# First output projection as seven block products, two chains of weight sums that begin behind x, and a last normalisation on three engines

## The chip, the cores and the metric

One core of a Trainium2 chip runs the kernel. The metric is the device time in microseconds (us) of one execution. Engines: PE (TensorE, matmuls), DVE (VectorE), ACT (ScalarE), POOL (GpSimd) and SP (SyncE, which here only issues transfers). Each engine carries out its own instructions in the order of the program; between engines they wait on semaphores. A transfer (DMA) is issued by an engine, waits there for what it depends on, and then runs on 16 DMA engines that all queues share.

## The reference

Two layers over x (512 tokens by 2048 channels), float32; each ends with `x <- LayerNorm(alpha*x + mixer(x))`.

```python
# layer 0 (even): attention half and Mamba-2 (SSD) half, then one output projection
hcat = x @ w_in
y_att = rms_norm(diff_attention(q, k, v, lam), subln_g) * (1 - lam_init) * silu(g_att)   # 1024 channels
y = ssd_chunked(xs * dt, a * dt, b, c) + d_skip * xs
y_ssm = rms_norm(y * silu(z), per group of 512) * ssm_norm_g                              # 1024 channels
y0 = concatenate([y_att, y_ssm]) @ w_out            # 512x2048 by 2048x2048: the first output projection
# layer 1 (odd): pooling mixer over four channel groups
y1 = (grouped(pool(v)) + b_grp) * scale * silu(g) @ w_out2                                # the second one
```

## The kernel before

Every float32 product is split: a value is written as `hi + lo` (line 113: ACT copies `hi` rounded to fp32r, DVE subtracts to get `lo`), and `mm3` (line 103) issues three matmuls, hi\*hi, hi\*lo, lo\*hi. Weights come as units of 128x1024 (512 KB): `unit` (line 117) loads one from SP's queue into one of three `raw` buffers and splits it; it is placed ahead of its program position by a priority. A scheduler then sets each engine's final order from its own model of times; the order of the text is only its priority.

Stages, in order: the B/C block of the SSD input (its results are the four tiles `bc`); projections of the token-major columns in five groups (`xs_group`, line 220); eight blocks of `xs` with the SSD steps woven in; the gate z; `ssm_norm` (line 445) scales y by `rs`, a reciprocal root that POOL computes with a power (line 452), and PE transposes the scaled y; eight attention heads; the first output projection (lines 611 to 700); `ln1`; the pooling mixer in four groups; the second output projection as seven block products instead of eight (lines 878 to 953); `finish`, the last LayerNorm.

Work beside the matmuls is fed by lanes: generators that yield estimated microseconds, advanced by each `mm3`.

The seven products of the second projection need sums of weight blocks. `presum` (line 191) makes them by transfers alone, on POOL's queue: it loads a block into `t`, adds others by accumulating transfers, and stores the four sums T1 to T4 to DRAM; a second tile `t3` makes T3. One call issues 10 transfers of 512 KB (2 loads, 4 accumulating, 4 stores); 8 calls make 80. `PACE` (7.0) is what each step yields to `lane3`.

The first output projection before is plain: 4 column groups of 512, 8 units each, 4 token tiles, 2 contraction blocks per unit, three matmuls each: 4 x 8 x 4 x 2 x 3 = 768 matmuls of 512 columns, into the tiles `po`.

`finish(t)` (line 922): two DVE operations per 512 columns (lines 926, 928), then a store by SP.

Of the kernel before, what the change touches and what calls it, by code (L numbers as in the profile page):

```python
# [29 lines left out]
PACE = 7.0  # L30
# [57 lines left out]
def hybrid_trunk(ctx: ExitStack, tc: tile.TileContext, xT, xtok, wa, wg, wo, prm, con, lnp, out, dbg=None):  # L88
# [6 lines left out]
    lane, lane2, lane3 = Lane(), Lane(), Lane()  # L95
# [7 lines left out]
    def mm3(o, sh, sl, mh, ml, start, stop, more=False):  # L103

        nc.tensor.matmul(o, sh, mh, start=start, stop=False, skip_group_check=more)  # L105
        nc.tensor.matmul(o, sh, ml, start=False, stop=False, skip_group_check=more)  # L106
        nc.tensor.matmul(o, sl, mh, start=False, stop=stop, skip_group_check=more)  # L107
        us = 3 * mh.free_size() / 2400.0
        lane.tick(us)
        lane2.tick(us)  # L110
        lane3.tick(us)
# [74 lines left out]
    def wsrc(c, j, cp, ch):  # L186
        return wo[((cp * 2 + c) * 2 + j) * 4 + ch]

    tsum = {}

    def presum(cp, ch, pool):
# [10 lines left out]
        nc.gpsimd.dma_start(t, wsrc(0, 1, cp, ch), accum_op=ALU.add)  # L202
        nc.gpsimd.dma_start(t3, wsrc(1, 1, cp, ch), accum_op=ALU.add)
# [4 lines left out]
        nc.gpsimd.dma_start(t, wsrc(1, 1, cp, ch), accum_op=ALU.add)  # L208
# [3 lines left out]
        nc.gpsimd.dma_start(t, wsrc(1, 0, cp, ch), accum_op=ALU.add)  # L212
# [5 lines left out]
    with ExitStack() as l1:  # L218
# [14 lines left out]
        with ExitStack() as sd:  # L233
# [207 lines left out]
        a2 = l1.enter_context(tc.tile_pool(name="att2", bufs=2))  # L441
# [157 lines left out]
        lane3.flush()  # L599
        yh, yl = newT("y")  # L600

        def y_ready(k):
            if k < 8:
                if k >= 6:
                    lane.flush()
                split(yh[k], yl[k], yTa[0][:, k])
            else:
                split(yh[k], yl[k], yTs[:, k - 8])


        un = next_units(32)
        ks = list(range(8, 16)) + list(range(8))
        first = [bank("mm", f"po{t}") for t in range(NT)]
        for u in range(8):
            hi, lo = unit(un[u])
            for j in range(2):
                y_ready(ks[2 * u + j])
            for t in range(NT):
                for j in range(2):
                    k = ks[2 * u + j]  # L620
                    mm3(first[t], yh[k][:, ts(t)], yl[k][:, ts(t)], hi[:, j * 512:(j + 1) * 512],
                        lo[:, j * 512:(j + 1) * 512], u + j == 0, u == 7 and j == 1)
        if dbg is not None and "yTa" in dbg:
            nc.sync.dma_start(dbg["yTa"], yTa[0])
            nc.sync.dma_start(dbg["yTs"], yTs)

    def out_mm(pt, t, u, ah, al, ks, hi, lo):
        for j in range(2):
            k = ks[2 * u + j]
            mm3(pt, ah[k][:, ts(t)], al[k][:, ts(t)], hi[:, j * 512:(j + 1) * 512],  # L630
                lo[:, j * 512:(j + 1) * 512], u + j == 0, u == 7 and j == 1)

    def out_cols(toks, units, ah, al, ks, evac):

        pt = {t: bank("mm", f"po{t}") for t in toks}
        for u in range(8):
            hi, lo = unit(units[u])
            for t in toks:
                out_mm(pt[t], t, u, ah, al, ks, hi, lo)
                if u == 7:  # L640
                    evac(t, pt[t])

    def moments(pool, stt):
        mv = pool.tile([P, 2], F32, tag="mv", name="mv", bufs=4)
        nc.vector.bn_aggr(mv, stt)
        rstd = pool.tile([P, 1], F32, tag="rstd", name="rstd", bufs=4)
        nc.vector.tensor_scalar(rstd, mv[:, 1:2], EPS, None, op0=ALU.add)
        nc.gpsimd.tensor_tensor(rstd, rstd, nhalf[:, :1], ALU.pow)
        return mv[:, 0:1], rstd

    def cs(cg):
        return slice(cg * 512, (cg + 1) * 512)

    with ExitStack() as l2:
        x1p = l2.enter_context(tc.tile_pool(name="x1p", bufs=1))
        x1h = [x1p.tile([P, 4, T], F32R, tag=f"h{k}", name=f"x1h{k}") for k in range(4)]
        x1l = [x1p.tile([P, 4, T], F32R, tag=f"l{k}", name=f"x1l{k}") for k in range(4)]
        oc = l2.enter_context(tc.tile_pool(name="oc", bufs=1))
# [3 lines left out]
        zp = zs.enter_context(tc.tile_pool(name="zp", bufs=2))  # L662
# [4 lines left out]
        def evac1(cg):  # L667
            def ev(t, pt):
                xs = xp[t][:, cs(cg)]
                nc.vector.scalar_tensor_tensor(xs, in0=xs, scalar=ALPHA, in1=pt, op0=ALU.mult, op1=ALU.add)  # L670
                nc.vector.bn_stats(stt[t][:, cg], xs)
            return ev
# [51 lines left out]
        v0 = act.tile([P, 4, T], F32, tag="l2", name="v0")  # L724
        gts = act.tile([P, 4, T], F32, tag="h2", name="gt0")
# [7 lines left out]
        H0, H1 = slice(0, 256), slice(256, 512)  # L733

        with ExitStack() as mix:
            p2 = mix.enter_context(tc.tile_pool(name="pool2", bufs=2))
            yr = []
            x1d = dram.tile([NT, P, D], F32, name="x1d")

            def residual():  # L740

                for cg in range(4):
# [4 lines left out]
                    for t in range(NT):  # L747
# [3 lines left out]
                        nc.gpsimd.dma_start(x1d[t][:, cs(cg)], xs)  # L751
# [3 lines left out]
            for g, w in enumerate(WINDOWS):  # L755
                plh = act.tile([P, 4, T], F32R, tag="h3", name="plh")
                pll = act.tile([P, 4, T], F32R, tag="l3", name="pll")
# [35 lines left out]
                yr.append(act.tile([P, 2, 2, T], F32, tag=("h0", "l0", "h1", "l1")[g], name=f"yr{g}"))  # L793
# [24 lines left out]

        op = l2.enter_context(tc.tile_pool(name="op", bufs=1))
        xp = [x1p.tile([P, D], F32, tag=f"h{t}", name=f"xq{t}") for t in range(NT)]
# [4 lines left out]
        def combo(pool, tags, src):  # L830

            hi, lo = (pool.tile([P, 8, 256], F32R, tag=t, name=f"c{t}") for t in tags)
            for g in range(4):
                q = slice(2 * g, 2 * g + 2)
                split(hi[:, q], lo[:, q], src(g, q))
            return hi, lo
# [4 lines left out]
        def summed(first, second, sub):  # L841
            def src(g, q):
                o = sraw[:, q]
                nc.vector.tensor_tensor(o, first(g, q), second(g, q), ALU.subtract if sub else ALU.add)
# [7 lines left out]

        def prod(o, a, b, ch, start, stop):

            for i in range(2):
                for uu in range(2):
                    u = 2 * ch + uu
                    mm3(o[i], a[0][:, u, ts(i)], a[1][:, u, ts(i)], b[0][:, uu * 512:(uu + 1) * 512],
                        b[1][:, uu * 512:(uu + 1) * 512], start and u == 0, stop and u == 7, True)

        def col(cp, j):
            return cs(2 * cp + j)

        def acc(t, cp, j, pt, sub=False, done=False):
            xs = xp[t][:, col(cp, j)]
# [3 lines left out]

        def pair(tag):  # L870
            if tag == "mm":
                return [bank("mm", "pY") for _ in range(2)]
            if tag == "aux":
                return [bank("aux", "pZ") for _ in range(2)]
            b = bank2("pZ2")
            return [b[:, 0], b[:, 1]]
# [3 lines left out]
        for cp in range(2):  # L880
            for ch in range(4):
                prod(Y[cp], a11, unit(wsrc(0, 0, cp, ch)), ch, True, False)
                prod(Z[cp], s1, unit(tsum[1, cp, ch]), ch, True, False)
            if cp == 0:
                s2 = combo(x1p, ("l0", "l1"), summed(sr, A11, True))
# [150 lines left out]
```

## Time and profile before

| | |
|---|---|
| median of 3 runs | 1440.17 us (1436.61 to 1444.72) |
| profiled execution, its time | 1442.42 us |
| its span (first to last instruction) | 1439.9 us |
| PE busy | 1409.6 us (98%) |
| DVE busy | 818.7 us (57%) |
| ACT busy | 548.5 us (38%) |
| POOL busy | 96.6 us (7%) |

The page gives busy time by engine, 40 slices of the span, the transfers by queue, the chain that ended last, the costliest groups and the transfers by line. Windows, timelines, waits and the transfers of a stretch are then asked of the trace. A matmul's duration in a row (0.39 us) overlaps the next one's; the distance between two starts is what one costs in a dense stretch. "idle before" in brackets is how long the engine had nothing to do, and what it waited for.

### The profile page before, as it was taken

What the parts mean: (1) busy time and instruction counts of PE and PEld (TensorE: products, weight loads), DVE (VectorE), ACT (ScalarE), POOL (GpSimd) and SP (SyncE); (2) the same over time, 40 slices, a digit from 0 to 9 for tenths busy, and PEclk for the clock granted to TensorE, in tenths of its full rate; (3) what the DMA queues carried; (4) which work ended last, traced back from release to release, by engine and by line L of the source; (5) the groups of instructions that cost most, each with busy time, mean ns of one, the idle gap of its engine ahead of it and who ended that gap; (6) DMA issues with size and microseconds to landing.
All of it is one profiled execution on the core that took longest, in us unless ns stands there. A gap on an engine that the chain in (4) does not pass through costs nothing.

```text
span 1439.9 us, 17608 instructions
## 1 busy us (share of the span) xinstructions
PE 1409.6 (98%) x6893; PEld 1192.2 (83%) x6893; DVE 818.7 (57%) x1198; ACT 548.5 (38%) x906; POOL 96.6 (7%) x150
## 2 busy tenths in 40 slices
PE   8999999999999999999999999999999999999994
PEld 6898899888888888888888889978888888888883
DVE  4755764542555555557335677865445346476678
ACT  4332433432544444446223456323232232345440
POOL 1112111110000000000000000110000000200101
PEclk9999999999999999999999999999999999999997
DMA  9999867763222222222545555663333333466764
GB/s 326 268 270 248 226 175 198 190 174 104 88 84 78 80 82 80 82 82 80 159 134 148 190 176 167 216 210 109 94 96 99 94 101 99 145 225 192 244 203 150
DMA packets 65266, 221.97 MB, mean 154 GB/s; under 512 B 7584, under 2 KB 7712, under 8 KB 65184
## 3 DMA queue, kind: packets, MB, share of 16 engines
q1 hardware_dynamic: 49824, 166.32, 36.6%
q0 software_dynamic: 15360, 54.53, 14.3%
q8 instruction: 54, 0.88, 0.2%
q14 instruction: 28, 0.23, 0.0%
HBM read 195.66 MB, written 25.17 MB: 153 GB/s over the span
## 4 chain that ended last, share of the span: by engine, by line
PE 91%; DVE 4%; DMA 3%; issue 1%; ACT 1%; SPq 0%; POOL 0%; DVEq 0%; ACTq 0%; POOLq 0%
PE pg L107 8%; PE pg L105 8%; PE pg L106 8%; PE po L107 4%; PE po L105 4%; PE po L106 4%; PE pv L107 3%; PE pv L106 3%; PE pv L105 3%; PE pq L107 2%; PE pq L105 2%; PE pgt L107 2%; PE pk L107 2%; PE pk L106 2%; PE pq L106 2%; PE pxs L105 2%
## 5 line engine op out<-in xcount | busy, mean ns | idle before, releaser
L115 DVE TENSOR_TENSOR lo<-raw,hi 128x1024 fp32r<-128x1024 f32 (+3 forms) x298 | 353.9, 1188 | 421.3 <-ACT hi L114 419.5
L114 ACT CAST hi<-raw 128x1024 fp32r<-128x1024 f32 (+3 forms) x298 | 304.9, 1023 | 581.8 <-PE po L107 97.0
L105 PE MATMUL pg<-hi,xh 128*128 128x346 f32 (+2 forms) x320 | 114.9, 360 | 0.0
L107 PE MATMUL pv<-x1h,lo 128*128 128x512 f32 (+1 forms) x320 | 111.9, 350 | 2.4 <-DVE lo L115 2.4
L105 PE MATMUL pv<-x1h,hi 128*128 128x512 f32 (+1 forms) x320 | 112.0, 350 | 0.0
L106 PE MATMUL pg<-lo,xh 128*128 128x346 f32 (+2 forms) x320 | 111.7, 349 | 0.0
L106 PE MATMUL pv<-x1l,hi 128*128 128x512 f32 (+1 forms) x320 | 111.6, 349 | 0.0
L107 PE MATMUL pg<-hi,xl 128*128 128x346 f32 (+2 forms) x320 | 111.5, 348 | 0.0
L107 PE MATMUL pg<-x1h,lo 128*128 128x512 f32 (+1 forms) x288 | 105.6, 367 | 0.1
L105 PE MATMUL pg<-x1h,hi 128*128 128x512 f32 (+1 forms) x288 | 105.6, 367 | 0.0
L106 PE MATMUL pg<-x1l,hi 128*128 128x512 f32 (+1 forms) x288 | 105.3, 366 | 0.0
L105 PE MATMUL po<-hi,yh 128*128 128x512 f32 x256 | 101.1, 395 | 0.0
L107 PE MATMUL po<-hi,yl 128*128 128x512 f32 x256 | 100.0, 390 | 0.0
L106 PE MATMUL po<-lo,yh 128*128 128x512 f32 x256 | 99.7, 389 | 0.0
L107 PEld LDWEIGHTS pv<-x1h,lo 128*128 128x128 f32 x320 | 61.2, 191 | 10.2 <-DVE lo L115 2.8
L106 PEld LDWEIGHTS pv<-x1l,hi 128*128 128x128 f32 x320 | 61.3, 191 | 7.5
L105 PEld LDWEIGHTS pv<-x1h,hi 128*128 128x128 f32 x320 | 61.2, 191 | 7.5
L106 PEld LDWEIGHTS pg<-lo,xh 128*128 128x128 f32 x320 | 60.4, 189 | 6.4 <-issue 1.4
L105 PEld LDWEIGHTS pg<-hi,xh 128*128 128x128 f32 x320 | 60.3, 188 | 6.3 <-issue 1.4
L107 PEld LDWEIGHTS pg<-hi,xl 128*128 128x128 f32 x320 | 60.2, 188 | 5.2
L107 PEld LDWEIGHTS pg<-x1h,lo 128*128 128x128 f32 x288 | 54.3, 189 | 9.1 <-DVE lo L115 0.3
L105 PEld LDWEIGHTS pg<-x1h,hi 128*128 128x128 f32 x288 | 54.4, 189 | 8.7
(281 smaller groups left out, 2845.9 us busy)
## 6 DMA issues: line engine op xcount, KB each, us to landing
raw<-in_wa SPq DMA_DIRECT2D x202, 512.0 KB, 3.6
pre<-in_wo POOLq DMA_DIRECT2D x48, 512.0 KB, 6.6
t<-pre POOLq DMA_DIRECT2D x32, 512.0 KB, 4.2
raw<-t SPq DMA_DIRECT2D x32, 512.0 KB, 3.3
raw<-in_wo SPq DMA_DIRECT2D x24, 512.0 KB, 3.7
raw<-in_wg SPq DMA_DIRECT2D x16, 512.0 KB, 4.6
raw<-in_wg SPq DMA_DIRECT2D x16, 346.0 KB, 5.2
xp<-in_xtok SPq DMA_DIRECT2D x16, 256.0 KB, 6.5
```

What stands on the lines that cost most here:

```text
L105: nc.tensor.matmul(o, sh, mh, start=start, stop=False, skip_group_check=more)
L106: nc.tensor.matmul(o, sh, ml, start=False, stop=False, skip_group_check=more)
L107: nc.tensor.matmul(o, sl, mh, start=False, stop=stop, skip_group_check=more)
L114: nc.scalar.copy(hi, src)
L115: nc.vector.tensor_tensor(lo, src, hi.bitcast(F32), ALU.subtract)
```

## The change

1. **First output projection.** It becomes seven products of blocks (half of the tokens, half of the contraction, half of the columns), as the second one is: `a11`, `s1`, `s4`, `s2`, `a12`, `s3`, `a22`. A product is 2 column halves x 4 units x 2 token tiles x 2 blocks x 3 = 96 matmuls of 512 columns. Operands are sums of halves of `yTs` (SSD) and `yTa` (attention); results are added to `xp` by `acc1` on DVE.
2. **Weight sums for both projections.** `presum` runs 16 times, in two lanes (`sums2`) with tiles of their own (`pre0`, `pre30`, `pre1`, `pre31`), `PACE` 13. The first call of either chain copies a column of `bc[0]` into its tiles, so that it starts behind the B/C block.
3. **Last normalisation.** `finish` uses ACT (scale and shift), DVE (times gain) and an accumulating transfer of POOL into `out`, which was filled with the bias earlier by four transfers. The a22 product stands ahead of a12, and `finish(2)`, `finish(3)` are pushed earlier.
4. Buffers move between pools to make room.

```diff
-PACE = 7.0
+PACE = 13.0
...
-    lane, lane2, lane3 = Lane(), Lane(), Lane()
+    lane, lane2, sums2 = Lane(), Lane(), (Lane(), Lane())
...
-        t = pool.tile([P, 1024], F32, tag="pre", name="pre")
-        t3 = pool.tile([P, 1024], F32, tag="pre3", name="pre3")
-        nc.gpsimd.dma_start(t, wsrc(0, 0, cp, ch))
-        nc.gpsimd.dma_start(t3, wsrc(0, 1, cp, ch))
+        t = pool.tile([P, 1024], F32, tag=f"pre{n}", name="pre")
+        t3 = pool.tile([P, 1024], F32, tag=f"pre3{n}", name="pre3")
+        if after is not None:
+
+            nc.gpsimd.tensor_copy(t[:, :1], after)
+            nc.gpsimd.tensor_copy(t3[:, :1], after)
+        nc.gpsimd.dma_start(t, wsrc(w, 0, 0, cp, ch))
+        nc.gpsimd.dma_start(t3, wsrc(w, 0, 1, cp, ch))
         yield PACE
...
-            pre = keep
-            for cp in range(2):
-                for ch in range(4):
-                    lane3.push(presum(cp, ch, pre))
+            for w, tsum in ((wo1, ts1), (wo2, ts2)):
+                for i in range(8):
+                    sums2[i % 2].push(presum(w, tsum, i // 4, i % 4, keep, i % 2,
+                                             bc[0][:, :1] if w is wo1 and i < 2 else None))
...
-        lane3.flush()
...
+        a11 = half(0, "a11")
+        eight(a11, lambda u: yTs[:, u:u + 2, H0])
+        Y = [pair("mm"), pair("mm")]
+        for cp in range(2):
+            for ch in range(4):
+                prod(Y[cp], a11, unit(wsrc(wo1, 0, 0, cp, ch)), ch, True, False)
...
+        Z = [pair("aux"), pair("sc")]
+        for cp in range(2):
+            for ch in range(4):
+                prod(Z[cp], s1, unit(ts1[1, cp, ch]), ch, True, False)
...
+            for i in range(2):
+                acc1(i, cp, 0, Y[cp][i])
+                acc1(2 + i, cp, 1, Z[cp][i])
...
+        for l in sums2:
+            l.flush()
+        for cp in range(2):
+            for ch in range(4):
+                prod(Y[cp], a22, unit(ts1[4, cp, ch]), ch, False, True)
...
+                    with tc.issue_after(spill[-1].ins):
+                        for t in range(NT):
+                            nc.gpsimd.dma_start(out[0, ts(t)], lnp[1, 1].partition_broadcast(P))
...
-                nc.vector.scalar_tensor_tensor(xs, in0=xs, scalar=mu, in1=g1[0][:, cs(cg)],
-                                               op0=ALU.subtract, op1=ALU.mult)
-                nc.vector.scalar_tensor_tensor(xs, in0=xs, scalar=rstd, in1=g1[1][:, cs(cg)],
-                                               op0=ALU.mult, op1=ALU.add)
-                nc.sync.dma_start(out[0, ts(t), cs(cg)], xs)
+                nc.scalar.activation(xs, xs, AF.Identity, scale=rstd, bias=nm)
+                nc.vector.tensor_tensor(xs, xs, g1[:, cs(cg)], ALU.mult)
+                nc.gpsimd.dma_start(out[0, ts(t), cs(cg)], xs, accum_op=ALU.add)
                 yield 2.5
```

What the scheduler makes of it. POOL's queue at the start, before: `pre` and `pre_472` are the tiles `t` and `t3` of the first call, and a bracket names what the instruction waits for (`DMASW0` to `DMASW7` are the transfers of this queue in turn).

```order
L199 DMA pre<-in_wo 128x1024
L200 DMA pre_472<-in_wo 128x1024
L202 DMA pre<-in_wo 128x1024 [waits DMASW0_49]
L203 DMA pre_472<-in_wo 128x1024 [waits DMASW1_49]
L195 DMA t_00_608<-pre 128x1024 [waits DMASW2_49]
L195 DMA t_00_610<-pre_472 128x1024 [waits DMASW3_49]
L208 DMA pre<-in_wo 128x1024 [waits DMASW4_49]
```

And now:

```order
L236 COPY pre<-bc_98 128x1 [waits DVE_49]
L237 COPY pre_472<-bc_98 128x1
L236 COPY pre<-bc_98 128x1
L237 COPY pre_478<-bc_98 128x1
L238 DMA pre<-in_wo 128x1024 [waits Pool_49]
L239 DMA pre_472<-in_wo 128x1024 [waits Pool_49]
L238 DMA pre<-in_wo 128x1024 [waits Pool_49]
L239 DMA pre_478<-in_wo 128x1024 [waits Pool_49]
L241 DMA pre<-in_wo 128x1024 [waits DMASW0_49]
L242 DMA pre_472<-in_wo 128x1024 [waits DMASW1_49]
```

Four copies that wait for DVE stand ahead, and four tiles are in work in place of two: a transfer waits for the one issued four before it, not two.

POOL's queue where the weight sums end and the power of `ssm_norm` (`rs`) stands, before (rows 83 to 88 of the queue, the 80 transfers being rows 6 to 85):

```order
L195 DMA t_13_4105<-pre 128x1024 [waits DMASW4_49]
L212 DMA pre<-in_wo 128x1024 [waits DMASW5_49]
L195 DMA t_13_4252<-pre 128x1024 [waits DMASW6_49]
L452 ISA
L452 TENSOR_TENSOR rs<-rs,nhalf 128x4 [waits DVE_49,PE_49]
L452 TENSOR_TENSOR rs<-rs,nhalf 128x4 [waits DVE_49]
```

And now (rows 166 to 172, the 160 transfers being rows 10 to 169; the last 31 of them wait for the one issued two before):

```order
L251 DMA pre<-in_wo 128x1024 [waits DMASW2_49]
L251 DMA pre<-in_wo 128x1024 [waits DMASW3_49]
L230 DMA t_12_6602<-pre 128x1024 [waits DMASW4_49]
L230 DMA t_13_6620<-pre 128x1024 [waits DMASW5_49]
L492 ISA
L492 TENSOR_TENSOR rs<-rs,nhalf 128x4 [waits DVE_49,PE_49]
L492 TENSOR_TENSOR rs<-rs,nhalf 128x4 [waits DVE_49]
```

Before and now, all weight sums stand ahead of `rs`: 80 before, 160 now. The powers of the attention heads (line 617) come behind it as well.

DVE's queue at the scaling of y by `rs`, before (`lo` is the second half of a weight unit's split):

```order
L451 TENSOR_SCALAR rs<-ssq 128x4 [waits DVE_49,Activation_49]
L455 TENSOR_SCALAR y<-y,rs 128x512 [waits Pool_49]
L455 TENSOR_SCALAR y<-y,rs 128x512 x3
L115 TENSOR_TENSOR lo<-raw,hi 128x1024 [waits DMAHW2_49,Activation_49]
L115 TENSOR_TENSOR lo<-raw,hi 128x1024 [waits DMAHW3_49,Activation_49]
L115 TENSOR_TENSOR lo<-raw,hi 128x1024 [waits DMAHW4_49,Activation_49]
```

And now:

```order
L491 TENSOR_SCALAR rs<-ssq 128x4 [waits DVE_49,Activation_49,Pool_49]
L116 TENSOR_TENSOR lo<-raw,hi 128x1024 [waits DMAHW2_49,Activation_49]
L495 TENSOR_SCALAR y<-y,rs 128x512 [waits Pool_49]
L495 TENSOR_SCALAR y<-y,rs 128x512 x3
L116 TENSOR_TENSOR lo<-raw,hi 128x1024 [waits DMAHW3_49,Activation_49]
L116 TENSOR_TENSOR lo<-raw,hi 128x1024 [waits DMAHW4_49,Activation_49]
```

One `lo` moves ahead of the scaling; all later ones stay behind it. On PE, the first transpose of the scaled y stands at row 1478 before and at row 1499 now, 21 matmuls of 512 columns later.

## Rows read from the trace of the kernel before

**Rows 1.** The page, part 1: busy us, share of the span, instructions.

```profile
PE 1409.6 (98%) x6893; PEld 1192.2 (83%) x6893; DVE 818.7 (57%) x1198; ACT 548.5 (38%) x906; POOL 96.6 (7%) x150
```

**Rows 2.** Page, parts 3 and 4: POOL's queue (MB, share); chain by engine.

```profile
q0 software_dynamic: 15360, 54.53, 14.3%
...
PE 91%; DVE 4%; DMA 3%; issue 1%; ACT 1%; SPq 0%; POOL 0%; DVEq 0%; ACTq 0%; POOLq 0%
```

**Rows 3.** Timeline of PE: last matmuls of the first output projection (start, us).

```profile
857.68 0.39 PE L105 MATMUL po<-hi,yh 128*128 128x512 f32 x1
...
859.49 0.39 PE L107 MATMUL po<-hi,yl 128*128 128x512 f32 x1
```

**Rows 4.** Timeline of POOL: the only chain near its end, then the norm's power.

```profile
288.45 0.53 POOL L199 DMA_DIRECT2D pre<-in_wo  x1 [2.64 <-DMA t<-pre]
...
320.24 0.55 POOL L195 DMA_DIRECT2D t<-pre  x1 [5.36 <-DMA pre<-in_wo]
326.11 1.04 POOL L452 TENSOR_TENSOR rs<-rs,nhalf 128x4 f32<-128x4 f32 x1 [5.31 <-DVE rs L451]
```

**Rows 5.** Timeline of DVE round that power, and the first block of `bc`.

```profile
58.16 0.68 DVE L246 SCALAR_TENSOR_TENSOR bc<-cth,acc 128x512 f32<-128x512 f32 x1
...
325.80 0.16 DVE L451 TENSOR_SCALAR rs<-ssq 128x4 f32<-128x4 f32 x1
327.18 1.67 DVE L455 TENSOR_SCALAR y<-y,rs 128x512 f32<-128x512 f32 x4 [1.22 <-POOL rs L452]
```

**Rows 6.** Timeline of PE: the transposes that read the scaled y.

```profile
327.96 1.28 PE L461 MATMUL pyt<-kc,y 128*128 128x128 f32 x4
```

**Rows 7.** DMA queues, 60 to 155 us (share of 16 engines; issues, us to landing).

```profile
q0 software_dynamic: 4195, 15.28, 62.7%
q1 hardware_dynamic: 2694, 9.34, 31.1%
...
pre<-in_wo POOLq DMA_DIRECT2D x18, 512.0 KB, 7.3
...
t<-pre POOLq DMA_DIRECT2D x11, 512.0 KB, 5.1
```

**Rows 8.** DMA queues, 200 to 320 us.

```profile
q0 software_dynamic: 3456, 12.58, 46.1%
q1 hardware_dynamic: 3153, 10.01, 25.6%
...
pre<-in_wo POOLq DMA_DIRECT2D x13, 512.0 KB, 5.6
...
t<-pre POOLq DMA_DIRECT2D x10, 512.0 KB, 3.4
```

**Rows 9.** Windows: busy of PE, PEld, DVE, ACT, POOL, clock, DMA share, GB/s.

```profile
10.00:15.00 5.00, 4.18 (x11) 3.09 (x12) 3.28 (x5) 3.00 (x5) 0.85 (x1) 0.66 1.03 318
20.00:40.00 20.00, 18.94 (x83) 15.06 (x82) 9.99 (x12) 8.77 (x12) 3.39 (x5) 1.00 1.03 378
676.70:860.00 183.30, 183.30 (x842) 152.09 (x841) 100.09 (x136) 69.01 (x99) 2.17 (x3) 1.00 0.51 158
```

**Rows 10.** What PE waited for, 0 to 60 us (total, times, longest).

```profile
PE pbc L105 <- ACT hi L114: 3.4, 2, 2.8
PE pbc L107 <- DVE lo L115: 1.2, 2, 0.7
```

**Rows 11.** DVE by line and form, whole span (count, busy, mean ns).

```profile
L115 DVE TENSOR_TENSOR lo<-raw,hi 128x1024 fp32r<-128x1024 f32 x270 | 330.1, 1223 | 397.7 <-ACT hi L114 396.3
L866 DVE TENSOR_TENSOR xq<-xq,pY 128x512 f32<-128x512 f32 x20 | 12.8, 679 | 0.0
L806 ACT ACTIVATE yr<-y,osc 128x512 f32<-128x512 f32 x16 | 11.6, 724 | 22.8 <-DVE y L804 22.7
```

**Rows 12.** Timelines of the tail: last matmul (PE), last steps behind it (DVE).

```profile
1420.19 0.39 PE L107 MATMUL pY<-wl,cl 128*128 128x512 f32 x1
...
1434.80 1.41 DVE L928 SCALAR_TENSOR_TENSOR xq<-xq,rstd,lnbl 128x512 f32<-128x512 f32 x2
```

More of the change, by code (lines that the diff above doesn't have):

```diff
@@ L110, in mm3 @@
         lane2.tick(us)
-        lane3.tick(us)
+        for l in sums2:
+            l.tick(us)
     def split(hi, lo, src):
@@ L184, in parameters, with prod, pair, cs @@
         nc.vector.tensor_scalar(nega, nega, -1.0, None, op0=ALU.mult)
[L186 to L191, printed above, removed]
+    H0, H1 = slice(0, 256), slice(256, 512)
+    def prod(o, a, b, ch, start, stop, toks=(0, 1)):
+        for i in toks:
+            for uu in range(2):
+                u = 2 * ch + uu
+                mm3(o[i], a[0][u][:, ts(i)], a[1][u][:, ts(i)], b[0][:, uu * 512:(uu + 1) * 512],
+                    b[1][:, uu * 512:(uu + 1) * 512], start and u == 0, stop and u == 7, True)
+    def pair(tag):
+        if tag == "sc":
+            b = bank2("pZ2")
+            return [b[:, 0], b[:, 1]]
+        return [bank(tag, "pY" if tag == "mm" else "pZ") for _ in range(2)]
+    def cs(cg):
+        return slice(cg * 512, (cg + 1) * 512)
+    def moments(pool, stt):
+        mv = pool.tile([P, 2], F32, tag="mv", name="mv", bufs=4)
+        nc.vector.bn_aggr(mv, stt)
+        rstd = pool.tile([P, 1], F32, tag="rstd", name="rstd", bufs=4)
+        nc.vector.tensor_scalar(rstd, mv[:, 1:2], EPS, None, op0=ALU.add)
+        nc.gpsimd.tensor_tensor(rstd, rstd, nhalf[:, :1], ALU.pow)
+        return mv[:, 0:1], rstd
+    def wsrc(w, c, j, cp, ch):
+        return w[((cp * 2 + c) * 2 + j) * 4 + ch]
+    ts1, ts2 = {}, {}
+    def presum(w, tsum, cp, ch, pool, n, after=None):
         def to(n, t):
@@ L597, in hybrid_trunk @@
         g_block(HEADS - 1)
-        lane3.flush()
[L600 to L658, printed above, removed]
+        def half(tag, name):
+            hi, lo = (act.tile([P, 8, 256], F32R, tag=f"{p}{tag}", name=f"{name}{p}") for p in "hl")
+            return [hi[:, u] for u in range(8)], [lo[:, u] for u in range(8)], hi, lo
@@ L665, in hybrid_trunk, with acc1 @@
                 nc.sync.dma_start(xp[t][:, cs(cg)], xtok[t][:, cs(cg)])
-        def evac1(cg):
-            def ev(t, pt):
-                xs = xp[t][:, cs(cg)]
+        begun = set()
+        def acc1(t, cp, j, pt, sub=False, done=False):
+            cg = 2 * cp + j
+            xs = xp[t][:, cs(cg)]
+            if (t, cg) in begun:
+                nc.vector.tensor_tensor(xs, xs, pt, ALU.subtract if sub else ALU.add)
+            else:
+                assert not sub
+                begun.add((t, cg))
@@ L674, in ln1, with behind @@
+        x1l = [act.tile([P, 4, T], F32R, tag=f"l{k}", name=f"x1l{k}") for k in range(4)]
+        def behind(qs, src):
+            for u in range(0, 8, 2):
+                q, k = qs[u // 4], u % 4
+                split(x1h[q][:, k:k + 2, H1], x1l[q][:, k:k + 2, H1], src(u))
+            return tuple([x[qs[u // 4]][:, u % 4, H1] for u in range(8)] for x in (x1h, x1l))
         def ln1(t):
@@ L828, in hybrid_trunk, with two, sums, diff @@
                 nc.gpsimd.dma_start(xp[t][:, cs(cg)], x1d[t][:, cs(cg)])
[L830 to L832 removed]
+        def two(a):
+            return [a[0][:, u] for u in range(8)], [a[1][:, u] for u in range(8)]
+        def sums(pool, tags, src):
+            a = tuple(pool.tile([P, 8, 256], F32R, tag=t, name=f"c{t}") for t in tags)
             for g in range(4):
                 q = slice(2 * g, 2 * g + 2)
[L835 to L836 removed]
+                split(a[0][:, q], a[1][:, q], src(g, q))
+            return two(a)
         def block(c, h):
             return lambda g, q: yr[g][:, :, c, h]
[L841 removed]
+        def diff(first, second, op):
             def src(g, q):
                 o = sraw[:, q]
[L844 removed]
+                nc.vector.tensor_tensor(o, first(g, q), second(g, q), op)
                 return o
@@ L851, in hybrid_trunk @@
         A11, A21, A12, A22 = block(0, H0), block(0, H1), block(1, H0), block(1, H1)
[L853 to L862, printed above, removed]
+        a11, s1 = two(a11), two(s1)
         def acc(t, cp, j, pt, sub=False, done=False):
-            xs = xp[t][:, col(cp, j)]
+            xs = xp[t][:, cs(2 * cp + j)]
             nc.vector.tensor_tensor(xs, xs, pt, ALU.subtract if sub else ALU.add)
```

183 lines of the change are left out of this document (114 added, 69 removed).

## The prediction

> **What bounds the kernel now.** I read the page first: PE is busy for 98% of the span [rows 1], and the chain that ended last is PE for 91% [rows 2]. So the reader should look for places where PE's own work shrinks, and for places where something else makes PE wait. I then read what PE waited for: between the start and the end there is little, 4.6 us in the first stage, where the B/C block waits for x and its weights [rows 10], and a tail behind the last matmul [rows 12].
>
> The third view is POOL's timeline, because the change puts twice as many transfers on its queue. It shows that the queue is in order and blocks: each weight-sum transfer waits there for an earlier one to land, the last is issued at 320.24, and the power for `rs` comes behind it at 326.11 [rows 4]. It was not late: its input from DVE was ready at 325.96, so POOL had been free for some 5 us [rows 4, 5]. DVE then waited 1.22 us for it with the four scalings of y, and the transposes on PE followed at 327.96 [rows 5, 6]. This place decides the prediction: before, the 80 transfers end 5 us ahead of the power.
>
> The last view is the transfers by stretch. From 60 to 155 us, POOL's queue holds 62.7% and SP's 31.1% of the 16 engines, together 93.8% [rows 7]. The fullest stretch, x loading, shows a share of 1.03 [rows 9]. So there is next to no room in that stretch for a second chain.
>
> **The change, part by part.**
>
> *Seven products.* 768 matmuls become 7 x 96 = 672, 96 fewer. One costs the distance of two starts: from 857.68 to 859.49 are 8 steps, 0.227 us each [rows 3]. 96 x 0.227 = 21.8 us off, all on PE's path. In return DVE's work there grows while the stage shrinks from 183.3 us to some 161.5. Before, DVE is busy 100.1 of 183.3 us [rows 9]. Added are 8 units split (1.22 us), 12 more additions into `xp`, 16 sums of operands and 12 more splits of operands (0.68 each) [rows 11]: 10 + 27 = 37 us, so 137 of 161.5. That is 85% on average, more in the parts where `s2` and `s4` are formed. I add 4 us, between 0 (units are split ahead, and additions can lie late) and 15 (40% of the added work comes through).
>
> *Start behind x.* The sums no longer share the transfers with x. The most that this can give back is the 4.6 us of waits [rows 10] and a little clock; the least is nothing. I take 4.
>
> *Last normalisation.* The last matmul starts at 1420.19, so PE ends at 1420.6; DVE then works up to 1436.2, since it adds the last blocks and runs two `finish` side by side, four steps of two operations each [rows 12]; the span ends at 1439.9, a tail of 19.3 us. Now one `finish` is four steps of ACT (0.72 us, the nearest ACT row) with DVE (0.68) behind each [rows 11]. Behind the last matmul: addition and statistics 1.4, mean and power 2, four steps 3.6, issue and landing of the last accumulating transfer 5 to 7 (7.3 is the landing of 512 KB under load [rows 7], 256 KB here). 12 to 14 us, so 7 less, between 3 and 10.
>
> *Twice the weight sums, and the power behind them.* That is the large term. All 160 transfers stand ahead of `rs` on POOL's queue, as the 80 did; the larger `PACE` doesn't hold them apart.
>
> Their start: `bc[0]` is written at 58.84 [rows 5]; 4 us earlier and four short copies later, 55.
>
> The price of one of 512 KB, in time of all 16 engines: over the whole run 14.3% of 1439.9 us for 54.53 MB (104 times 0.524 MB) is 1.98 us [rows 2]; from 60 to 155 us 62.7% of 95 us for 29 is 2.05 [rows 7]; from 200 to 320 us 46.1% of 120 us for 23 is 2.40 [rows 8]. The mix stays (2 loads, 4 accumulating, 4 stores per call). I take 1.98, since the others hold time in which a packet shares its engine with units, and keep 2.40 as the upper end. The units hold 31.1% and 25.6% [rows 7, 8], 28% on average; PE needs them until it stops, about 271 us x 0.28 = 76 us.
>
> The first 129 transfers have four in work at a time; I let them fill the engines to the share of 1.03 [rows 9]: (129 x 1.98 + 76) / 1.03 = 322 us, to 377. The last 31 run as two chains. One chain alone holds 46.1% [rows 8], two then 92%: 31 x 1.98 / 0.92 = 67 us, to 444. With 2.40 and two chains that step as the single one does (31.8 us for 7 steps, 4.5 each [rows 4], 15.5 x 4.5 = 70) it is (310 + 76) / 1.0 = 386, 441, then 511. That is the upper end. The lower one, 380, is what a fifth less per transfer at greater depth would give: (129 x 1.58 + 76) / 1.03 = 272, and 31 x 1.58 / 0.92 = 53.
>
> Behind the waiting power stand, in order: DVE's scaling of y; behind it on DVE all further `lo` halves of weight units, so PE gets no more weights; and PE's transposes. One unit more is split ahead of the scaling than before, so PE runs on for 21 matmuls (4.8 us): it stops at 327.96 - 4 + 4.8 = 329. It starts again at 444 + 1.04 + about 1 = 446. That is 117 us of idle PE, and 2 more for the clock: from 10 to 15 us, where PE had waited before, the mean granted clock is 0.66 of 2.4 GHz, which costs 1.7 us there [rows 9]; I take 2, between 0 and 5.
>
> *The rest* (filling `out` early, other pools) lies beside PE work in stretches that are not short of transfers; I take nothing for it.
>
> Sum, on the profiled execution's span: 1439.9 - 21.8 + 4 - 4 - 7 + 117 + 2 = 1530.1. The execution itself took 2.5 more than its span, and the median of the runs is 2.2 below it, which about cancel: 1530.
>
> **The rivals.**
>
> *A: the transfers speed up at depth, and nothing stalls (faster).* Four in work instead of two could raise the rate rather than queue. 160 x 0.524 MB are 84 MB, and the units until 326 about 24 (9.34 MB in 95 us, 10.01 in 120 [rows 7, 8]); 108 MB at 378 GB/s [rows 9] take 286 us, to 341, a stall of 14 us; with a little more, 400 GB/s, 325 and none. Then the time is 1439.9 - 28.8 = 1411 (1425 with the 14). It decides below a last landing at 329. For it: the stretch with 378 GB/s. Against it: that stretch was mostly plain loads, and with accumulating transfers the engines were 93.8% full at far less.
>
> The Trainium skill, DMA: Bandwidth & Descriptors, section "Anatomy of one DMA — SWDGE (gpsimd) path", fits a transfer from POOL as a fixed 2.0 us plus its bytes at 436 GB/s, that is 1.2 us of data for 512 KB, accumulating or not. By that rule A is what happens (an estimate: 160 x 1.2 us plus the units end near 305). The trace disagrees: transfers into `pre` land in 5.6 us with a quiet queue, stores in 3.4 [rows 8].
>
> *B: half of it.* The engines go to 300 to 350 GB/s for this mix: 108 MB take 309 to 360 us, the end lies at 364 to 415, the stall is 37 to 88 us, the time 1450 to 1500. The upper part lies in my range.
>
> *C: PE is also starved earlier*, by units that come late in the full stretch. The 3 raw buffers cover it before. It would move idle time ahead of the stop and not add to it, as the end at 444 is set by the transfers: 1530 to 1540.
>
> *D: DVE becomes the bound in the first output projection*: 15 us instead of 4, 1541 with the stall.
>
> **How the numbers follow.** Forecast with C and D as its variants and the upper part of B: 0.82. A: 0.10. B below 1465: 0.04, half of it within 0.5% of before. Above 1575 (a last landing past 489, as the end at 511 is): 0.04, since the row of 2.40 is the one with the most room on the engines. The range 1465 to 1575 leaves out some 0.18. About 0.5% is what a measurement of this kernel can tell from no change; faster by more than that has 0.10, within it 0.02, slower 0.88.
>
> **What would show it.** In the profile after: POOL with 160 transfers up to about 444 and the power behind; a wait of DVE's scaling for POOL of over 100 us; two to three empty slices of PE near 330 to 446; transfers at about full share up to there, and POOL idle but for powers afterwards. The first output projection should be some 162 us long with 672 matmuls, the first stage without the 4.6 us of waits, and the tail 12 us. I'm wrong if the last sum is issued before 330, or if PE goes on through it.

## The result and the profile after

The kernel after takes 1530.12 us (median of 4 runs, 1525.85 to 1530.81), the one before on the same chip 1442.12 (4 runs, 1436.61 to 1444.72): a ratio of 1.061, 95% interval 1.057 to 1.065. The forecast was 1530. The profiled execution took 1525.85 with a span of 1524.0; the spans of the other three are 1528 to 1529. So by its own sum, 1530.1 on the span, the forecast was 6 us above the profile that is read here.

Page, part 1, part 2 (40 slices of 38.1 us), and parts 3 and 4 [rows 1, 2]:

```profile
PE 1387.9 (91%) x6797; PEld 1173.6 (77%) x6797; DVE 839.1 (55%) x1230; ACT 574.0 (38%) x942; POOL 164.7 (11%) x250
...
PE   9999999950049999999999999999999999999995
...
PEclk9999999985569999999999999999999999999998
DMA  7699999999853222222237655577433333375658
...
q0 software_dynamic: 29440, 103.82, 25.5%
...
PE 68%; DMA 25%; issue 3%; DVE 2%; POOL 1%; ACT 0%; POOLq 0%; DVEq 0%
DMA pre<-in_wo 15%; DMA t<-pre 9%; PE pg L107 4%; PE pg L106 4%; PE pg L105 4%; PE pY L106 4%; PE pY L105 4%; PE pY L107 4%; PE pv L107 3%; PE pv L106 3%; PE pv L105 3%; PE pZ L106 2%; PE pZ L105 2%; PE pZ L107 2%; PE pq L105 2%
```

PE has 96 instructions fewer and is busy 21.7 us less. But slices 9 to 12 hold a hole, DMA stays at 8 or 9 through most of it, and a quarter of the chain that ended last is the weight sums (`pre`, `t`). What was waited for (total, times, longest):

```profile
DVE y L495 <- POOL rs L492: 114.4, 2, 113.3
PE pyt L501 <- DVE y L495: 112.2, 1, 112.2
```

The timelines of POOL, DVE and PE at that place [rows 4 to 6]:

```profile
52.83 0.18 POOL L236 COPY pre<-bc 128x1 f32<-128x1 f32 x1 [52.38 <-DVE bc L285]
...
363.52 0.53 POOL L230 DMA_DIRECT2D t<-pre  x1 [2.44 <-DMA pre<-in_wo]
...
436.60 0.55 POOL L230 DMA_DIRECT2D t<-pre  x1 [1.94 <-DMA pre<-in_wo]
437.25 1.08 POOL L492 TENSOR_TENSOR rs<-rs,nhalf 128x4 f32<-128x4 f32 x1
```

```profile
319.72 0.16 DVE L491 TENSOR_SCALAR rs<-ssq 128x4 f32<-128x4 f32 x1
438.36 1.68 DVE L495 TENSOR_SCALAR y<-y,rs 128x512 f32<-128x512 f32 x4 [113.31 <-POOL rs L492]
```

```profile
326.39 0.39 PE L107 MATMUL pg<-hi,xl 128*128 128x512 f32 x1
439.00 0.66 PE L501 MATMUL pyt<-kc,y 128*128 128x128 f32 x2 [112.21 <-DVE y L495]
```

The input of the power is ready at 319.9; POOL issues the 129th sum transfer at 363.52, the 160th and last at 436.60, and then the power, whose row names no wait: POOL itself was the wait. Before, the power named DVE as its releaser.

Windows (busy of PE, PEld, DVE, ACT, POOL; clock, DMA share, GB/s) [rows 9]:

```profile
300.00:360.00 60.00, 26.78 (x117) 21.46 (x115) 12.66 (x16) 10.02 (x17) 18.27 (x27) 0.77 0.99 280
360.00:390.00 30.00, 0.00 (x0) 0.00 (x0) 0.00 (x0) 0.00 (x0) 9.21 (x14) 0.50 0.96 255
390.00:440.00 50.00, 1.00 (x4) 0.85 (x5) 1.64 (x4) 0.00 (x0) 14.11 (x20) 0.50 0.82 212
440.00:460.00 20.00, 20.00 (x88) 16.61 (x87) 3.71 (x4) 5.59 (x7) 0.00 (x0) 0.89 0.23 60
784.90:946.70 161.80, 161.40 (x744) 133.48 (x743) 132.20 (x183) 84.39 (x120) 3.44 (x3) 1.00 0.62 205
```

During the stall every other engine is empty; the granted clock goes to 0.50 (1.2 GHz) and is 0.89 in the first 20 us behind it. The last row is the whole first output projection, 161.8 us with DVE busy for 82% of it.

The shift by place in the program (us, starts of matmuls; the right pair is the version e6 below, in which only the stall is taken away):

| place | before | after | shift | e6 | shift |
|---|---|---|---|---|---|
| first `pg` (first stage) | 56.09 | 50.01 | -6.1 | 48.99 | -7.1 |
| first `pyt` (behind `rs`) | 327.96 | 439.00 | +111.0 | 321.1 | -6.9 |
| first matmul of first output projection | 676.8 | 784.9 | +108.1 | 668.9 | -7.9 |
| first `pv` (behind it) | 859.7 | 946.7 | +87.0 | 830.7 | -29.0 |
| last `pgr` (`L105`) | 1267.4 | 1349.2 | +81.8 | 1231.7 | -35.7 |
| last matmul | 1420.19 | 1504.65 | +84.5 | 1387.16 | -33.0 |
| end of span | 1439.9 | 1524.0 | +84.1 | 1406.9 | -33.0 |

### The profile page after: what moved, and what is told of

Read it like the earlier page. It is cut to its first block, busy times and chain, and to the rows that moved or that the text cites. A ratio compares the mean times of both kernels' runs of the same rounds, so it can differ in the third digit from the quotient of the medians.

```text
span 1524.0 us, 17595 instructions
## 1 busy us (share of the span) xinstructions
PE 1387.9 (91%) x6797; PEld 1173.6 (77%) x6797; DVE 839.1 (55%) x1230; ACT 574.0 (38%) x942; POOL 164.7 (11%) x250
## 4 chain that ended last, share of the span: by engine, by line
PE 68%; DMA 25%; issue 3%; DVE 2%; POOL 1%; ACT 0%; POOLq 0%; DVEq 0%
DMA pre<-in_wo 15%; DMA t<-pre 9%; PE pg L107 4%; PE pg L106 4%; PE pg L105 4%; PE pY L106 4%; PE pY L105 4%; PE pY L107 4%; PE pv L107 3%; PE pv L106 3%; PE pv L105 3%; PE pZ L106 2%; PE pZ L105 2%; PE pZ L107 2%; PE pq L105 2%
## 5 line engine op out<-in xcount | busy, mean ns | idle before, releaser
L116 DVE TENSOR_TENSOR lo<-raw,hi 128x1024 fp32r<-128x1024 f32 (+3 forms) x306 | 363.8, 1189 | 380.7 <-ACT hi L115 379.0
L115 ACT CAST hi<-raw 128x1024 fp32r<-128x1024 f32 (+3 forms) x306 | 313.5, 1025 | 564.5 <-PE pg L107 93.9
L105 PE MATMUL pg<-hi,xh 128*128 128x346 f32 (+2 forms) x320 | 115.2, 360 | 0.0
L106 PE MATMUL pg<-lo,xh 128*128 128x346 f32 (+2 forms) x320 | 112.2, 351 | 0.0
L105 PE MATMUL pv<-x1h,hi 128*128 128x512 f32 (+1 forms) x320 | 111.3, 348 | 0.0
L501 PE MATMUL pyt<-kc,y 128*128 128x128 f32 x32 | 6.6, 335 | 112.2 <-DVE y L495 112.2
L105 PE MATMUL pg<-x1h,hi 128*128 128x512 f32 (+1 forms) x288 | 105.4, 366 | 0.0
L501 PEld LDWEIGHTS pyt<-kc,y 128*128 128x128 f32 x32 | 5.1, 175 | 114.0 <-issue 113.4
L105 PEld LDWEIGHTS pv<-x1h,hi 128*128 128x128 f32 x320 | 60.6, 189 | 7.6
L495 DVE TENSOR_SCALAR y<-y,rs 128x512 f32<-128x512 f32 x8 | 3.4, 484 | 114.4 <-POOL rs L492 114.4
L105 PEld LDWEIGHTS pg<-hi,xh 128*128 128x128 f32 x320 | 60.5, 189 | 6.4 <-issue 1.4
L105 PEld LDWEIGHTS pg<-x1h,hi 128*128 128x128 f32 x288 | 54.3, 189 | 8.8
```

What stands on the lines that cost most here:

```text
L115: nc.scalar.copy(hi, src)
L116: nc.vector.tensor_tensor(lo, src, hi.bitcast(F32), ALU.subtract)
L495: nc.vector.tensor_scalar(ysl, ysl, rs[:, t:t + 1], None, op0=ALU.mult)
L501: nc.tensor.transpose(pt[:, ts(t)], y[:, t, ts(b)], ident)
```

## The experiments

**e1 and e6, e10: both powers off POOL.** The sums, their order and their number stay; only the powers of `rs` and of the heads go to ACT and DVE.

```diff
-            nc.gpsimd.tensor_tensor(rs, rs, nhalf[:, :4], ALU.pow)
+            nc.scalar.activation(rs, rs, AF.Sqrt)
+            nc.vector.reciprocal(rs, rs)
...
-            nc.gpsimd.tensor_tensor(ss[:, 0], ss[:, 0], nhalf[:, :4], ALU.pow)
+            nc.scalar.activation(ss[:, 0], ss[:, 0], AF.Sqrt)
+            nc.vector.reciprocal(ss[:, 0], ss[:, 0])
```

> The reciprocal roots of the SSD norm and of the attention heads are made by ACT (square root) and DVE (reciprocal) in place of POOL's power; all 160 weight-sum transfers stay as they are, up to about 437 us. Theory Q (PE stops only because the power stands behind the sums in POOL's queue): PE's wait of 112 us is gone and the span is 1524 - 112 - 2 = 1410 us, up to 1420 with the table loads that ACT now needs. Rival S (the full DMA engines would stop PE anyway, since weight units come late while the sums still run): idle time of PE reappears in pieces between 326 and 440 us, span above 1470 us.

Measured: 1410.48 us (one run; before on that chip 1436.93). PE's waits over the whole run are these, and the sums still run, up to 462.57:

```profile
PE pg L107 <- DVE lo L116: 2.0, 2, 1.8
PE pbc L293 <- DVE nhalf L173: 1.5, 1, 1.5
PE px L751 <- DVE xp L745: 0.9, 2, 0.5
```

```profile
462.57 0.55 POOL L230 DMA_DIRECT2D t<-pre  x1 [3.84 <-DMA pre<-in_wo]
```

```profile
320.00:440.00 120.00, 119.96 (x572) 99.17 (x571) 55.88 (x93) 57.13 (x106) 31.24 (x45) 1.00 0.98 284
```

In the 120 us in which the kernel after stands still, PE works throughout beside a DMA share of 0.98. So the stall isn't a lack of weights: PE's units and two chains fit side by side, and only the place of the power on the queue cost it. (The run moves both kinds of power at once; the wait rows of the kernel after name the one of `rs`.) Timed again, twice:

> The version with both powers off POOL once more, timed in five rounds, so that the others of this call and the kernel before have it beside them: 1410 us, within 3 of it. If its single run was a lucky one, it comes out above 1415. It is the sum of the forecast without its stall: 1530 less 117 and 2 for the clock is 1411.

> The version with the powers off POOL as the measure for the two others of this call: 1408, within 2.

1408.25 (1407.69 to 1410.71; ratio to before 0.980, 0.977 to 0.983) and 1410.82 (0.981, 0.979 to 0.983). The first lies within the 3 us that it was given, the second 0.8 us outside its 2. This version beats both kernels.

**e2: the sums spread behind the powers.** Each sum transfer is ordered behind the last power issued so far.

```diff
...
+            with behind_pow():        # tc.issue_after(the last power of POOL)
                 nc.gpsimd.dma_start(d, t)
...
```

> Each weight-sum transfer is bound to stand on POOL's queue behind the last power issued before it in the program, so that PACE spaces the sums again. Q: the first power no longer waits (sums ahead of it: 46 transfers, done before 200 us), PE runs on, span near 1410 us, unless the last sums, which now run beside the first output projection, make weight units late (up to 10 us more). If the stall has another cause, 1524 us stays.

Measured: 1465.57 us (1464.47 to 1465.7; ratio 1.020, 1.018 to 1.021). The stall at `rs` is gone, as expected; the rest missed by some 50 us, because the sums now end at 889, run beside the first output projection and stand in front of other work. POOL's timeline, PE's longest wait, two windows, and the chain from 700 to 760 by line:

```profile
319.50 1.04 POOL L503 TENSOR_TENSOR rs<-rs,nhalf 128x4 f32<-128x4 f32 x1 [147.16 <-DVE rs L502]
```

```profile
888.62 0.55 POOL L235 DMA_DIRECT2D t<-pre  x1 [2.03 <-DMA pre<-in_wo]
889.19 1.18 POOL L215 TENSOR_TENSOR rstd<-rstd,nhalf 128x1 f32<-128x1 f32 x2
```

```profile
PE px L760 <- DVE xp L754: 22.4, 2, 22.0
```

```profile
720.00:740.00 20.00, 10.56 (x29) 7.12 (x29) 8.25 (x12) 5.00 (x8) 4.57 (x7) 0.75 1.05 319
860.00:880.00 20.00, 6.28 (x42) 5.58 (x40) 7.48 (x13) 4.66 (x7) 3.92 (x6) 0.66 0.93 290
```

```profile
by line: DMA raw<-t 47.7%; DMA raw<-in_wo 27.6%; DVE lo L120 6.2%; ACT hi L119 5.3%; PE pY L110 3.5%; PE pY L111 2.7%; PE pY L109 2.7%; PE pZ L110 1.8%; PE pZ L111 1.5%; PE pZ L109 1.5%; issue 0.5%; ACTq L119 0.2%
```

At 889 the same happens once more with `rstd` of the first normalisation: a power behind the last sums, 22.0 us of PE. And from 700 to 760 the first output projection has to wait for its own units: `raw<-t` and `raw<-in_wo` are 75% of the chain there. From its first matmul to the first `px` it takes 146.6 us, against 121.1 in e6 below. So late units, with the lower clock beside them (0.75 in the first window), cost some 25 us where the expectation allowed 10, and the rest of the 57 us above e6 (spans 1463.7 and 1406.9) comes at `rstd` and behind it. Spreading a stall along the queue moves it to the next small operation and to the units that the transfers now run beside.

**e3: twelve calls in place of sixteen.** Four calls are left out, and the second projection reads the sums of its first column half twice (its output is another).

```diff
-                for i in range(8):
+                for i in range(8 if w is wo1 else 4):
...
```

> Four of the 16 calls of the weight sums are left out (the sums of the second projection's second column half; its products read those of the first half instead, so the output is not the reference's). Q: the sums end at 55 + 0.75 x 382 = 341 us, PE idles 16 us in place of 112, span 1428 us. If the wait does not hang on the number of transfers ahead: 1524 us.

```profile
353.66 0.55 POOL L230 DMA_DIRECT2D t<-pre  x1 [2.07 <-DMA pre<-in_wo]
354.31 1.08 POOL L492 TENSOR_TENSOR rs<-rs,nhalf 128x4 f32<-128x4 f32 x1
```

Measured: 1447.37 us (one run), PE idle for 35.3 us where 16 was expected. The mechanism holds, the size missed by 19 us: the end of the sums by 13, and PE stopped at 320.8, 6 us earlier than in the kernel after. The end came 82.9 us earlier for 40 transfers fewer, 2.07 us each. Up to the 81st transfer the two kernels agree within 1 us (247.1, 247.9); from there to the 120th it takes 106.6 us here and 94.5 in the kernel after, and here the last 31 of all, which run as two chains, lie in this part and beside PE's units. That this is the reason fits, but no run shows it by itself.

**e4: all transfers plain.** The four accumulating ones of a call become loads (the sums aren't formed, the output is another).

```diff
-        nc.gpsimd.dma_start(t, wsrc(w, 0, 1, cp, ch), accum_op=ALU.add)
+        nc.gpsimd.dma_start(t, wsrc(w, 0, 1, cp, ch))
...
```

> All 160 transfers stay, but none accumulates: they are plain loads over the same tiles (so the sums are not formed). Q with the engines' time as the limit: an accumulating packet took about twice a plain one (327 against 159 ns), so 64 x 8 x 0.168 = 86 us less, the end of the sums near 351 us, PE idles 26 us, span 1438 us. Rival L (the limit is the latency of a chain's steps, four in work): a step of an accumulating transfer falls from 5.7 to 4.2 us, a call from 37.6 to 33, the end near 391 us, span 1478 us.

```profile
389.58 0.54 POOL L230 DMA_DIRECT2D t<-pre  x1 [1.94 <-DMA pre<-in_wo]
```

```profile
300.00:360.00 60.00, 25.81 (x112) 20.65 (x110) 12.66 (x16) 9.12 (x17) 14.83 (x28) 0.75 0.85 294
360.00:390.00 30.00, 0.00 (x0) 0.00 (x0) 0.00 (x0) 0.00 (x0) 7.42 (x15) 0.50 0.75 244
```

Measured: 1479.36 us (one run), PE idle for 66.2 us. The sums end 47.0 us earlier, as the rival said, not 86: once the engines have room (share 0.85, then 0.75), the steps of the chains set the pace. So two limits follow each other in the kernel after: the engines up to about 390 (share 0.99, then 0.96), and then, with two chains left and the share at 0.82, the steps.

**e7: the sums from 0.** e6 without the copies that hold the chains behind `bc[0]`.

```diff
-                                             bc[0][:, :1] if w is wo1 and i < 2 else None))
+                                             None))
```

> The version with both powers off POOL, and the weight sums without the copies that hold them behind the first block of bc: the two chains begin at 0, beside x and the first weights. Theory (the start behind x gives back the waits of the first stage, forecast 4 us): PE waits of 4 to 8 us in the first 60 us, two chains taking more of the engines there than the one of the kernel before, which cost it 4.6; the time 4 to 8 us above the other version of this call, some 1416. The sums end some 50 us earlier, at about 410, which changes nothing for PE. Rival (what went from the first stage is due to something else, and PE's start is set by x alone): the time is within 1.5 us of the other version.

Measured: 1432.52 us (11 runs, 1428.44 to 1437.14), 24 above e6, which was timed beside it; 20.1 by the spans (1427.0, 1406.9). Both expectations missed, the size by a factor of three to five. First a window (PE is busy for 4.6 of 10 us, at a DMA share of 1.04), then the chain that ended last (start, us):

```profile
20.00:30.00 10.00, 4.56 (x13) 2.86 (x13) 2.10 (x4) 2.80 (x4) 1.27 (x3) 0.83 1.04 296
```

```profile
6.44 22.34 DMA raw<-in_wa
...
31.14 15.27 DMA raw<-in_wa
```

A weight unit that lands in 6.5 us (median, 0 to 50 us, kernel after) takes 15.8 here, 12.9 in the kernel before, with one chain. The first `pg` starts at 67.69, against 48.99, 18.7 of the 20.1 us. So the start behind x is worth 20 us against the two chains that the change has, and some 6 against one chain, as the table's first row has it (that row compares the whole kernels; no run takes one chain by itself).

**e5, e8, e9: the end without accumulating into `out`.** All on e6. In e5 the fills of `out` go, a tile `b1` holds the bias, DVE adds it, SP stores; in e8 POOL adds it; in e9 `finish(2)` and `finish(3)` accumulate as before, and only the last two end as in e5.

```diff
...
-                nc.gpsimd.dma_start(out[0, ts(t), cs(cg)], xs, accum_op=ALU.add)
+                nc.vector.tensor_tensor(xs, xs, b1[:, cs(cg)], ALU.add)     # e8: nc.gpsimd
+                nc.sync.dma_start(out[0, ts(t), cs(cg)], xs)
```

> The version with both powers off POOL (square root on ACT, reciprocal on DVE), and the last normalisation without the accumulating transfer: the four fills of out are gone, the bias is loaded into a tile behind the gain, DVE adds it, SP stores. In the profile of the version with the powers off POOL the last step on DVE ends at 1398.9 and the span at 1408.7, 9.8 us later; in the kernel before these two lie 3.7 us apart (1436.2, 1439.9), and its stores by SP land in 2.4 us. Theory (the accumulating transfers at the very end are what ate the 7 us forecast for the tail): the last finish gets 4 additions of 0.69 more on DVE, 2.8 us, and the close shrinks from 9.8 to 3.7: 3 to 4 us less than the version with the powers off POOL of the same call, some 1406, and no share of the engines above 0.6 behind the last matmul. Rival (the tail is set by additions, statistics, mean and power, and the close of the program takes as long with any transfer): 2.8 us more, some 1413.

> As the version with plain stores, but POOL adds the bias in place of DVE, so that the 16 additions no longer stand on DVE's queue, where the ones of the first two finishes pushed the last blocks' additions back: nm of finish(0) came at 1393.06 there, at 1387.03 in the version that accumulates into out. Theory (the close of 3.6 us behind the last step is what a plain store costs, against 9.8, and DVE's queue ate the gain): nm of finish(0) is back near 1387, the last ACT step ends near 1396.5, DVE's product near 1397.2, POOL's addition at 1398 to 1399, then 3.6: 1402, 5 us below the version with the powers off POOL. POOL's addition on 128x512 is not in any trace so far. Rival (it costs 2 us or more, POOL being slower, and the power of finish(1) waits behind four of them): the end at 1406 or later, no gain.

> As the version with the powers off POOL, but only finish(2) and finish(3), which lie beside matmuls, accumulate into out; finish(0) and finish(1), which end the kernel, add the bias on DVE and store by SP. Theory (as for the other): DVE's queue ahead of the last blocks holds no more than before, nm of finish(1) comes at about 1393.5, four steps of 1.37 on DVE behind one ACT step of 0.73 end at 1399.8, then 3.6: 1403.5, 3 to 4 us below the version with the powers off POOL. Rival (finish(0) and finish(1) overlap on DVE, so that eight steps of 1.37 end the kernel: 1394 and 11 and 3.6): 1408, no gain.

Measured: e5 1409.43 (e6 beside it 1408.25), e8 1415.25 and e9 1409.26 (e10 beside them 1410.82). e5 and e9 gain nothing that their runs can tell, and e8 is some 4 us slower (1414.61 to 1416.84, against 1409.58 to 1411.58). The gains that the theories forecast (1406, 1402, 1403.5) came in none of the three, and the rivals of e8 and e9, no gain, came. From e5, `nm` of `finish(0)` and the last step on DVE:

```profile
1393.06 0.16 DVE L989 SCALAR_TENSOR_TENSOR nm<-mv,rstd 128x1 f32<-128x1 f32 x1 [0.41 <-POOL rstd L211]
...
1403.38 0.69 DVE L994 TENSOR_TENSOR xq<-xq,lnb 128x512 f32<-128x512 f32 x1
```

The close behind the last step is 3.6 us in e5 (1404.07, span 1407.7), as expected, in place of some 9.5. What it gave went to DVE: the additions of `lnb` stand ahead of the last blocks' additions, `nm` is 6 us later than in e6 (1387.03; PE ends 1.4 later), and the additions follow each step to the end. e8 put them on POOL, which takes 1726 ns for one, and slowed DVE's products beside it from 683 to 1101 ns (DVE and POOL by line and form, from 1384 us on; count, busy, mean ns):

```profile
L994 POOL TENSOR_TENSOR xq<-xq,lnb 128x512 f32<-128x512 f32 x16 | 27.2, 1726 | 10.0 <-DVE xq L993 10.0
```

```profile
L993 DVE TENSOR_TENSOR xq<-xq,lng 128x512 f32<-128x512 f32 x11 | 11.9, 1101 | 1.8 <-ACT xq L992 1.8
```

```profile
L996 DVE TENSOR_TENSOR xq<-xq,lng 128x512 f32<-128x512 f32 x11 | 7.2, 683 | 1.8 <-ACT xq L995 1.8
```

The first of these three is of e8's whole span, the second of e8, the third of e9. The Trainium skill, SBUF — State Buffer, section "SBUF: two separate sides", has POOL and DVE share a pair of ports, which one of them holds for a whole instruction; the two means agree with that in kind, and no run here takes the ports apart.

## Why the prediction was right

**The stall** was the step that decided, and it came for the reason given, in the order given: DVE's scaling of y, PE's transposes, and all further units behind them. Forecast 117, measured 112.2. Its parts: the 129th transfer at 377, measured 363.5 (nearly every piece of the term was a little too large: 1.91 us for a transfer where 1.98 was taken, as shown below; SP's queue, with the units, at 26.9% from 60 to 155 us and 23.7% from 200 to 320 where 31.1% and 25.6%, on average 28%, were; a start at 53.3 where 55 was; only the share was lower than taken, 0.99 from 300 to 360 for 1.03); the last 31 in 67, measured 73.1 (share 0.92 taken; 0.96 until 390 and 0.82 afterwards, where the steps rule). PE stopped at 326.8 in place of 329. The two misses of the end point against each other: 436.6 for 444. e1 shows the cause by itself: with the same sums ahead and the power elsewhere, the time is 1408 to 1411, 120 us less than after, where the sum without stall and clock gives 1411.

**The price of one transfer**, 1.98 us of all engines from the whole run [rows 2], holds at depth four. In the kernel after, first the two queues from 200 to 320 us, with four in work, then q0 from 330 to 440 us, for the most part with two, where PE's units add next to nothing:

```profile
q0 software_dynamic: 7014, 25.55, 77.4%
q1 hardware_dynamic: 3153, 10.16, 23.7%
...
q0 software_dynamic: 7012, 25.50, 89.9%
```

25.55 MB are 48.7 transfers of 0.524; 0.774 x 120 / 48.7 = 1.91 us with four in work, and 0.899 x 110 / 48.6 = 2.03 us in the later stretch. (The upper end of the forecast's price, 2.40, divides by the 23 issues of its row; by that row's 12.58 MB, 24 transfers, it is 2.30. The upper end's seven steps of a chain [rows 4] are six, 5.3 us each and not 4.5; the last 31 transfers took 73.1 us, 4.7 a step. The forecast of 1530 rests on neither.) With the price so little changed at depth four, rival A falls. The fit of the Trainium skill that the forecast cites behind A (DMA: Bandwidth & Descriptors, section "Anatomy of one DMA — SWDGE (gpsimd) path"), 2.0 us plus 1.2 of data, goes by the bytes alone, and the landings disagree with it: 8.1 us into `pre` from 200 to 320, 5.6 before [rows 8]. Rival B half came: from 60 to 300 us the rate did rise, to some 300 GB/s (259 before, from the two queues of [rows 7]), but that was not enough, and it fell to 255 and then 212 in the part with two chains. C and D didn't come: PE is busy for all of 60 to 300 us, and for 161.4 of the 161.8 us of the first output projection.

**The terms**, forecast and measured (from the table): start -4, -6.1; stall and clock 119, 114.2 (108.1 + 6.1); first output projection -21.8 + 4 = -17.8, -21.1. So DVE's load costs 0.7 of the 4 us, at 132 of 161.8 us busy where 137 was forecast: the units are split far enough ahead.

**The tail is the term that was mis-sized**: -7 forecast, from 19.7 (1439.9 less 1420.19) to 19.35 measured, -0.4. DVE, then POOL, behind the last matmul at 1504.65 [rows 12]:

```profile
1505.37 2.10 DVE L992 TENSOR_TENSOR xq<-xq,lng 128x512 f32<-128x512 f32 x3 [0.88 <-ACT xq L991]
1507.39 0.68 DVE L939 TENSOR_TENSOR xq<-xq,pZ 128x512 f32<-128x512 f32 x1
...
1508.59 0.69 DVE L941 BATCH_NORM_STATS2 bst<-xq 128x6 f32<-128x512 f32 x1
...
1511.66 2.81 DVE L992 TENSOR_TENSOR xq<-xq,lng 128x512 f32<-128x512 f32 x4 [0.88 <-ACT xq L991]
```

```profile
1512.81 3.52 POOL L993 DMA_DIRECT2D out<-xq  x4 [2.23 <-DVE xq L992]
```

The last addition starts 2.7 us after the last matmul does, behind three products of `finish(0)`, which the forecast's chain didn't have; statistics, mean, power and steps then take about as long as forecast and end at 1514.5; and the close takes 9.5 us, not 5 to 7. From 1480 to 1524 POOL's queue moves little and holds much:

```profile
q0 software_dynamic: 2304, 4.20, 66.0%
...
out<-xq POOLq DMA_DIRECT2D x16, 256.0 KB, 6.6
```

0.66 x 44 / 16 = 1.8 us of all engines for 256 KB: about what 512 KB of the sums cost on average (1.91 to 2.03), while the forecast scaled by bytes. The close by itself is shown by e5 (3.6 us); that it yields nothing as long as DVE has to add the bias, by e5 and e9.

**Not forecast**: the stretch from the first `pv` to the last `pgr` is 5.2 us shorter. Before, two windows lose PE time and show a lower granted clock; after, one window loses PE time and none shows a lower clock. Before, then after:

```profile
920.00:940.00 20.00, 18.37 (x128) 17.66 (x129) 18.27 (x33) 8.09 (x12) 3.21 (x6) 0.91 0.66 199
...
960.00:980.00 20.00, 18.14 (x73) 14.58 (x72) 16.58 (x23) 7.37 (x11) 2.16 (x4) 0.91 0.60 182
```

```profile
1000.00:1020.00 20.00, 17.65 (x144) 17.09 (x142) 17.08 (x32) 9.00 (x13) 3.24 (x6) 1.00 0.75 223
```

By these rows PE loses 3.5 us to idle time before and 3.6 to the clock (twice 0.09 of 20), and 2.35 after, which is 4.7 of the 5.2. And from the last `pgr` to the last matmul it takes 2.7 us longer, in e6 too, for the same 676 matmuls and with no wait of PE in the trace. PE's timeline shows where: in the four products whose operands are tiles of the pool `oc` (a11, s1, s3, a22), the starts of the 384 matmuls lie 0.2333 us apart, in the other three, and in all seven before, 0.2267. That is 2.5 us. The change opens that pool in another place (`side="right"`), which the forecast put at nothing ("other pools"). The causes of both weren't tried and stay open. With them the sum closes: 108.1 - 21.1 - 5.2 + 2.7 - 0.4 = 84.1.

**Luck.** The terms missed by -2.1 (start), -4.8 (stall and clock), -3.3 (first output projection), -5.2 and +2.7 (not forecast) and +6.6 (tail), together -6.1, the distance from 1530.1 to the span of 1524.0. They cancel in part, and that the median of the runs, 1530.12, falls on the forecast is luck.

## What to carry to other kernels

Read a queue as a line: before work is added to an engine that issues transfers, look for the small operation on that queue which another engine needs, and price all that stands ahead of it. Price the transfers twice, by the engines' time as long as the share is near 1 and by the steps of a chain once it isn't, since the later limit sets the end. The remedy here was to move two small powers to other engines, which turned 6% slower into 2% faster; reordering the queue sent the wait to the next small operation and made weight units late, and left it 2% slower than before.

## What the hardware showed that was not expected

- In the packet records of the traces an accumulating packet of 4 KB takes about 328 ns and a plain one 159: of POOL's 4 KB packets 32% take about 328 ns in the kernel after, 0.3% in e4, where no sum accumulates. The 2 KB packets that accumulate into `out` take 178, the plain ones that SP stores in e5 86.
- An accumulating transfer of 256 KB from SBUF into `out` holds all 16 engines for some 1.8 us, about as long as one of 512 KB of the sums does on average (1.91 to 2.03); a plain store of 256 KB by SP at the end of e5 lands in 2.5 us, against 6.6.
- POOL's addition on 128x512 takes 1726 ns, and DVE's product beside it 1101 ns in place of 683.
- Two chains of sums beside the loading of x cost 20 us (e7 against e6), one chain some 6 (before against after): a unit's landing went from 6.5 us without a chain to 12.9 with one and 15.8 with two.
